# A two-block transformer kernel on one core: the engines' queues laid by the context's timeline simulation

## The chip, the cores and the metric

The kernel runs on one core of a Trainium2 chip. Its time is the device time in microseconds (us) of one execution. Three runs of the kernel before took 1210.09 to 1213.05 us, with a median of 1211.94.

The core has engines that work side by side, each with a queue that it takes from the front: PE (matrix multiplications and transposes; the load of the stationary operand is listed as PEld), DVE (vector engine), ACT (scalar engine), POOL (a second engine for vector steps) and SP, whose queue does nothing but start DMAs. An instruction waits at the front of its queue until its operands are there and its buffer is free, and everything queued behind it waits too.

## The reference, cut to what matters

Two blocks are applied to `x` (512 tokens, 1024 wide, float32). The first one modulates the normalised input by a condition vector `c`, projects it, and runs two attentions with eight heads each:

```
mod = silu(c) @ w_ada + b_ada                      # shift, scale, gate
h = rms_norm(x, g_pre) * (1 + scale) + shift
qa, ka, va, fa, za, qb, kb, vb, zb = split(h @ w_in)
oa = forgetting_attention(qa, ka, va, fa) * silu(za)          # "fox"
ob = sliding_window_sink_attention(rope(qb), rope(kb), vb) * silu(zb)
x = x + gate * rms_norm(concat(oa, ob) @ w_out, g_post)
```

The second has three branches (a gated convolution with 31 taps, a differential attention with eight heads, a cross attention to 256 memory rows), merged by gates:

```
h = rms_norm(x, norm_g);  mem_h = rms_norm(mem, mem_norm_g)
u = silu(layer_norm(conv31(a * sigmoid(b)))) * silu(c_gate);   y_conv = u @ w_conv
a = softmax(q1 k1 + alibi) - lam * softmax(q2 k2 + alibi);     y_diff = (norm(a @ v) * silu(d_gate)) @ w_diff
y_mem = (softmax(norm(x_q) norm(k_mem)) @ v_mem * silu(x_gate)) @ w_x
x = x + (g0 * y_conv + g1 * y_diff + g2 * y_mem) @ w_out
```

## The kernel before, in words

*Matmuls in three passes.* Float32 products are split into a high and a low half and multiplied as high by high, high by low and low by high. The input `h` lies transposed in `hh` and `hl`. Each weight chunk goes through `load_w` (L158 to L176): a DMA from SP's queue into one of three `raw` buffers (L164), a rounding copy `wh` on ACT (L170), and the rest `wl = raw - wh` on DVE, every fourth one on POOL (L172). The matmuls read `wh` and `wl`: L198 with the weight as stationary operand (256-column chunks, outputs of 128 by 512 in transposed layout), L215 with `h` stationary (512-column chunks, natural layout), L207 for the keys of the sliding attention.

*The opening.* The memory keys (L421, `mem_k`, two halves of 16 matmuls each) and values (L431, `mem_v`) are products of the memory rows. The modulation is eight loads of 1 MB (`ada`, L328), each turned into column sums on DVE (`gemv`, L335 to L338), summed over the partitions by two tiny matmuls (L442) and made into a shift and a scale (`mod` L445, `gs` L446) with which ACT and POOL write one eighth of `hh` and `hl` (L448 to L450). The memory keys are normalised by a chain of ten small DVE steps (L228 to L237) and scaled (L512).

*The attentions.* In the first block the sliding attention has scores `sc` (L688, L689), transposes `tp` (L710) and products `pv` (L727); the fox attention L768 and L769, L784, L807, with DVE steps L771, L775, L787 and L813 between them; a row of gate sums (L751) is woven in. In the second block the differential attention has L1043 and L1044, L784, L1077, the cross attention L1187, L1208, L1230; its queries are normalised by POOL (`xqn`, L987) and transposed (L284). The 240 steps of the convolution (L933) are given to DVE at low priority. The gates, the projections of the branches and the output follow as long rows of L198 and L215.

*What sets the order.* The code emits instructions in an order of its own: a `Fill` object weaves pieces of the projections between the steps of the attentions. That order is a priority, which `low()` raises or lowers by a number for a part of the code (the convolution taps, the memory keys' scaling, small constants). The queues are then laid by the tile context: it goes through the instructions with a model of how long each one takes, and appends to each engine's queue the one of highest priority among those whose operands the model holds to be there. Which instruction stands ahead of which in a queue thus depends on the durations and waits of that model. The tile pools set how far an engine may run ahead: three banks for matmul outputs, two each for scores and transposes, one for attention products.

The context is opened in one line (L1471), which encloses the whole kernel function.

## Time and profile before

| | |
|---|---|
| median of 3 runs | 1211.94 us (1210.09 to 1213.05) |
| the profiled execution | 1207.46 us |
| its span, first to last instruction | 1205.6 us |
| mean granted clock of PE | 0.989 |
| PE, DVE, ACT, POOL busy | 1145.5, 920.8, 552.1, 206.7 us |
| DMA | 165.25 MB, 137 GB/s |

The span is what the profiler recorded between the first and the last instruction; the execution is slightly longer. Busy times are sums over an engine's instructions, so an idle engine shows as the difference to the span, but not why it idles: for that the waits are read, which name for each gap the event that ended last. The granted clock is the share of full speed (2.4 GHz) that PE was given.

### The profile page before, as it was taken

The page shows a single profiled execution, that of the slowest core. Times are in us where ns is not written, and L with a number is a line of the kernel's source. Part 1 is how long each engine was busy: PE and PEld are TensorE (multiplying, and loading weights), DVE is VectorE, ACT ScalarE, POOL GpSimd, SP SyncE. Part 2 cuts the span into 40 slices and gives each one's busy share as a digit, 9 for nine tenths or more (in the row PEclk, how much of TensorE's full clock was granted, in tenths as well). Part 3 has the DMA queues.
Part 4 walks back from the last instruction along what each step waited for, and adds up shares of the span by engine and source line. Part 5 has one row for each costly group of instructions (what it writes and reads, how often), then busy time and mean ns, then how long its engine had stood idle before and what let it go on. Part 6 is the DMA issues. An engine that isn't in the chain of part 4 may idle for free. (4 is left out here: it accounts for less than half of the span.)

```text
span 1205.6 us, 16186 instructions
## 1 busy us (share of the span) xinstructions
PE 1145.5 (95%) x5584; PEld 938.3 (78%) x5584; DVE 920.8 (76%) x2004; ACT 552.1 (46%) x1157; POOL 206.7 (17%) x158
## 2 busy tenths in 40 slices
PE   6979999999899999998999999989999999999998
PEld 3557787777677878887898787868788888888887
DVE  5597677789887699999999979978884488453342
ACT  4554567547665354444545443444432245242230
POOL 0534200000121212020111211121101131110110
PEclk9989999999999999999999899999999999999999
DMA  9475421353474423323233333233335856422232
GB/s 351 152 247 189 126 88 63 130 161 89 141 243 140 123 70 97 100 93 114 88 115 105 114 114 127 101 114 123 111 134 180 298 177 228 145 90 96 97 112 98
DMA packets 59873, 165.25 MB, mean 137 GB/s; under 512 B 7088, under 2 KB 11440, under 8 KB 58768
## 3 DMA queue, kind: packets, MB, share of 16 engines
q1 hardware_dynamic: 35824, 122.41, 30.9%
q10 hardware_dynamic: 23968, 41.82, 9.7%
q8 instruction: 44, 0.72, 0.2%
q14 instruction: 37, 0.30, 0.1%
HBM read 136.80 MB, written 20.58 MB: 131 GB/s over the span
## 5 line engine op out<-in xcount | busy, mean ns | idle before, releaser
L170 ACT CAST wh<-raw 128x512 fp32r<-128x512 f32 (+1 forms) x360 | 214.9, 616 | 195.5 <-PE mm L198 115.0
L172 POOL TENSOR_TENSOR wl<-raw,wh 128x512 fp32r<-128x512 f32 (+1 forms) x94 | 137.4, 1462 | 831.2 <-ACT wh L170 776.4
L172 DVE TENSOR_TENSOR wl<-raw,wh 128x512 fp32r<-128x512 f32 (+1 forms) x266 | 194.1, 745 | 91.7 <-ACT wh L170 88.2
L198 PE MATMUL mm<-hh,wh 128*128 128x512 f32 x640 | 255.7, 400 | 0.0
L198 PE MATMUL mm<-hh,wl 128*128 128x512 f32 x640 | 251.8, 393 | 0.0
L198 PE MATMUL mm<-hl,wh 128*128 128x512 f32 x640 | 251.6, 393 | 0.0
L933 DVE SCALAR_TENSOR_TENSOR cv<-u,vec,cv 128x512 f32<-128x512 f32 x240 | 195.1, 813 | 3.1
L198 PEld LDWEIGHTS mm<-hh,wl 128*128 128x128 f32 x640 | 121.4, 190 | 25.4
L198 PEld LDWEIGHTS mm<-hh,wh 128*128 128x128 f32 x640 | 121.5, 190 | 23.7
L198 PEld LDWEIGHTS mm<-hl,wh 128*128 128x128 f32 x640 | 121.4, 190 | 23.4
L215 PE MATMUL mm<-wh,hh 128*128 128x512 f32 x256 | 102.7, 401 | 0.6 <-ACT qkn L973 0.3
L215 PE MATMUL mm<-wh,hl 128*128 128x512 f32 x256 | 100.2, 391 | 0.0
L215 PE MATMUL mm<-wl,hh 128*128 128x512 f32 x256 | 100.1, 391 | 0.0
L198 PE MATMUL mm<-bh,wh 128*128 128x512 f32 x192 | 75.2, 392 | 0.0
L198 PE MATMUL mm<-bh,wl 128*128 128x512 f32 x192 | 74.7, 389 | 0.0
L198 PE MATMUL mm<-bl,wh 128*128 128x512 f32 x192 | 74.7, 389 | 0.0
L1048 ACT ACTIVATE dp<-dp,dst 128x128 f32<-128x128 f32 (+3 forms) x64 | 35.6, 558 | 70.3 <-DVE dst L1046 70.2
L215 PEld LDWEIGHTS mm<-wh,hh 128*128 128x128 f32 x256 | 48.2, 188 | 11.1 <-ACT qkn L973 1.0
L215 PEld LDWEIGHTS mm<-wh,hl 128*128 128x128 f32 x256 | 48.1, 188 | 10.4
L215 PEld LDWEIGHTS mm<-wl,hh 128*128 128x128 f32 x256 | 48.2, 188 | 9.1 <-DVE wl L172 0.3
L207 PE MATMUL mm<-wl,hh 128*128 128x256 f32 (+1 forms) x160 | 46.8, 293 | 4.9 <-DVE wl L172 4.9
L207 PE MATMUL mm<-wh,hl 128*128 128x256 f32 (+1 forms) x160 | 46.3, 290 | 0.0
(330 smaller groups left out, 2110.1 us busy)
## 6 DMA issues: line engine op xcount, KB each, us to landing
raw<-in_w_dram SPq DMA_DIRECT2D x88, 512.0 KB, 3.7
raw<-in_w_out_dram SPq DMA_DIRECT2D x24, 512.0 KB, 3.7
raw<-in_w2n_dram SPq DMA_DIRECT2D x24, 512.0 KB, 3.4
ada<-in_w_ada_dram SPq DMA_DIRECT2D x8, 1024.0 KB, 6.1
rawm<-in_w_mem_dram SPq DMA_DIRECT2D x8, 512.0 KB
raw<-in_w_mem_dram SPq DMA_DIRECT2D x8, 512.0 KB
raw<-in_w1n_dram SPq DMA_DIRECT2D x8, 512.0 KB, 4.3
ada<-in_w_gate_dram SPq DMA_DIRECT2D x8, 512.0 KB, 4.3
```

Source lines behind the costliest of these rows:

```text
L170: act.copy(out=wh, in_=raw[:, s])
L172: eng.tensor_tensor(out=wl, in0=raw[:, s], in1=f(wh), op=ALU.subtract)
L198: m = pe.matmul(out=ps, lhsT=a[:, c0:c0 + P], rhs=at(b, k), start=(n == 0 and i == 0), stop=(n == KT - 1 and i == 2))
L207: pe.matmul(out=ps, lhsT=at(a, k)[:, t * P:(t + 1) * P], rhs=b[:, 0:n], start=(start and m == 0 and i == 0), stop=(stop and m == len(order ...
L215: pe.matmul(out=ps, lhsT=at(a, k)[:, t * P:(t + 1) * P], rhs=b[:, 0:n], start=(m == 0 and i == 0), stop=(m == KT - 1 and i == 2))
L933: dve.scalar_tensor_tensor(out=a, in0=u[:, j:j + S], scalar=dw[:, m * 31 + j:m * 31 + j + 1], in1=a, op0=ALU.mult, op1=ALU.add)
L1048: act.activation(out=p_[:, :w], in_=p_[:, :w], func=AF.Exp, scale=-1.0, bias=st_[:, 0, n, m:m + 1], accum_out=st_[:, 1, n, m:m + 1])
```

## The change: another model lays the queues

The tile context is told to use its timeline simulation as the model when it lays the queues.

```diff
--- before.py
+++ after.py
@@ -1468,7 +1468,7 @@
     arrays = {f"in_{k}_dram": np.ascontiguousarray(v) for k, v in _layout(inputs).items()}
     aps = {k[3:-5]: nc.dram_tensor(k, a.shape, mybir.dt.from_np(a.dtype), kind="ExternalInput").ap() for k, a in arrays.items()}
     out = nc.dram_tensor("out_0_dram", (NT, P, 1024), F32, kind="ExternalOutput").ap()
-    with tile.TileContext(nc) as tc:
+    with tile.TileContext(nc, schedule_with_timeline_sim=True) as tc:
         two_block_kernel(tc, aps, out)
     r = run_bass_kernel_spmd(nc, [arrays], core_ids=[0])
     got = r.results[0]["out_0_dram"]
```

Instructions, operands, loads and buffers stay what they were: the same matrix instructions, the same 289 entries of SP's queue, the same steps on DVE, the same weights. Of 1887 buffers in the on-chip memory 225 get another address. What differs is the place of instructions in the queues. Three places follow; numbers behind a name tell tiles of one name apart, and x2 means two such rows in a run.

SP's queue in the opening, where the last loads of the modulation weights (`ada`), of the memory values (`raw` from w_mem) and the first chunk for the sliding attention's keys (`raw` from w1c) meet. Before:

```order
L328 DMA ada_321<-in_w_ada_dram 128x2048
L328 DMA ada_363<-in_w_ada_dram 128x2048
L164 DMA raw_580<-in_w_mem_dram 128x1024
L164 DMA raw_590<-in_w_mem_dram 128x1024
L328 DMA ada_365<-in_w_ada_dram 128x2048
L328 DMA ada_367<-in_w_ada_dram 128x2048
L164 DMA raw_783<-in_w1c_dram 128x528
L164 DMA raw_793<-in_w1c_dram 128x528
L164 DMA raw_803<-in_w1c_dram 128x528
L164 DMA raw_813<-in_w1c_dram 128x528
```

Now:

```order
L328 DMA ada_321<-in_w_ada_dram 128x2048
L164 DMA raw_580<-in_w_mem_dram 128x1024
L328 DMA ada_363<-in_w_ada_dram 128x2048
L164 DMA raw_590<-in_w_mem_dram 128x1024
L164 DMA raw_783<-in_w1c_dram 128x528
L164 DMA raw_793<-in_w1c_dram 128x528
L164 DMA raw_803<-in_w1c_dram 128x528
L328 DMA ada_365<-in_w_ada_dram 128x2048
L328 DMA ada_367<-in_w_ada_dram 128x2048
L164 DMA raw_813<-in_w1c_dram 128x528
```

The loads ada_365 and ada_367 have moved behind three of the four loads of w1c, and ada_363 behind raw_580.

PE's queue in the sliding attention, at the scores of its seventh block (sc_1941 to sc_1956, tokens of one block against keys), the transposes of the block before (tp_1979, tp_1986, of spt_1860) and a product (pv_1969). Before, with a gate projection (mm_1924) around:

```order
L688 MATMUL sc_1946<-kb11_1205,qs_1723 128x256
L689 MATMUL sc_1946<-kbl1_1206,qs_1723 128x256
L727 MATMUL pv_1969<-sph_1900,vbh_781 64x512
L727 MATMUL pv_1969<-spl_1901,vbh_781 64x512
L688 MATMUL sc_1951<-kb11_1205,qs_1731 128x256
L689 MATMUL sc_1951<-kbl1_1206,qs_1731 128x256
L727 MATMUL pv_1969<-sph_1900,vbl_782 64x512
L688 MATMUL sc_1956<-kb11_1205,qs_1734 128x256
L689 MATMUL sc_1956<-kbl1_1206,qs_1734 128x256
L710 MATMUL tp_1979<-cst_79,spt_1860 128x128 x4
L710 MATMUL tp_1986<-cst_79,spt_1860 128x128 x4
```

Now, with a projection of the fox attention's values (mm_2274) around:

```order
L215 MATMUL mm_2274<-wh_2158,hl_84 128x512
L688 MATMUL sc_1946<-kb11_1205,qs_1723 128x256
L689 MATMUL sc_1946<-kbl1_1206,qs_1723 128x256
L710 MATMUL tp_1979<-cst_79,spt_1860 128x128
L710 MATMUL tp_1986<-cst_79,spt_1860 128x128
L710 MATMUL tp_1979<-cst_79,spt_1860 128x128
L710 MATMUL tp_1986<-cst_79,spt_1860 128x128
L710 MATMUL tp_1979<-cst_79,spt_1860 128x128
L710 MATMUL tp_1986<-cst_79,spt_1860 128x128
L710 MATMUL tp_1979<-cst_79,spt_1860 128x128
L710 MATMUL tp_1986<-cst_79,spt_1860 128x128
L688 MATMUL sc_1951<-kb11_1205,qs_1731 128x256
```

The four scores no longer stand together; pv_1969 has gone ahead of them, the transposes of the earlier block come between sc_1946 and sc_1951, and the bulk matmuls ahead are those of a later chunk.

PE's queue in the cross attention, at the transposes (tp_8248, tp_8255) of the normalised queries xqn_7879. Before, in the midst of the gate projection mm_8233:

```order
L198 MATMUL mm_8233<-hh_83,wl_8157 128x512
L198 MATMUL mm_8233<-hh_83,wh_8156 128x512
L198 MATMUL mm_8233<-hl_84,wh_8156 128x512
L284 MATMUL tp_8248<-cst_79,xqn_7879 128x128 x2
L284 MATMUL tp_8255<-cst_79,xqn_7879 128x128 x2
L198 MATMUL mm_8233<-hh_83,wl_8157 128x512
L198 MATMUL mm_8233<-hh_83,wh_8160 128x512
L284 MATMUL tp_8248<-cst_79,xqn_7879 128x128 x2
L284 MATMUL tp_8255<-cst_79,xqn_7879 128x128 x2
L198 MATMUL mm_8233<-hl_84,wh_8160 128x512
```

Now, in the midst of a later one, mm_8353:

```order
L198 MATMUL mm_8353<-hh_83,wh_8284 128x512
L198 MATMUL mm_8353<-hl_84,wh_8284 128x512
L198 MATMUL mm_8353<-hh_83,wl_8285 128x512
L284 MATMUL tp_8248<-cst_79,xqn_7879 128x128 x2
L198 MATMUL mm_8353<-hh_83,wh_8290 128x512
L198 MATMUL mm_8353<-hl_84,wh_8290 128x512
L198 MATMUL mm_8353<-hh_83,wl_8291 128x512
L198 MATMUL mm_8353<-hh_83,wh_8290 128x512
L198 MATMUL mm_8353<-hl_84,wh_8290 128x512
L284 MATMUL tp_8255<-cst_79,xqn_7879 128x128
L284 MATMUL tp_8248<-cst_79,xqn_7879 128x128 x2
L284 MATMUL tp_8255<-cst_79,xqn_7879 128x128 x3
```

The rest of mm_8233, a whole further output (mm_8298) and the first half of mm_8353 have moved ahead of the transposes.

## Rows read from the trace of the kernel before

**Rows 1.** The page, part 1: busy us and share of the span.
```profile
PE 1145.5 (95%) x5584; PEld 938.3 (78%) x5584; DVE 920.8 (76%) x2004; ACT 552.1 (46%) x1157; POOL 206.7 (17%) x158
```

**Rows 2.** Windows by stage: length, busy per engine (instructions), clock, DMA share, GB/s.
```profile
0.00:105.00 105.00, 81.94 (x338) 56.30 (x338) 74.53 (x190) 52.52 (x101) 33.78 (x40) 0.95 0.68 248
105.00:215.70 110.70, 108.96 (x538) 86.80 (x537) 82.41 (x218) 66.97 (x166) 21.58 (x20) 1.00 0.31 98
215.70:321.00 105.30, 101.16 (x521) 79.46 (x522) 95.28 (x299) 64.16 (x158) 8.21 (x6) 1.00 0.37 118
321.00:451.60 130.60, 124.12 (x624) 102.67 (x624) 102.03 (x216) 68.18 (x136) 22.97 (x20) 1.00 0.47 156
451.60:724.20 272.60, 261.76 (x1429) 225.70 (x1428) 260.34 (x616) 129.69 (x286) 47.33 (x28) 0.98 0.33 105
724.20:870.00 145.80, 135.55 (x673) 113.01 (x671) 128.82 (x220) 62.05 (x129) 22.10 (x13) 0.98 0.33 113
870.00:1206.00 336.00, 331.99 (x1472) 274.34 (x1470) 177.40 (x250) 108.53 (x186) 50.77 (x33) 1.00 0.45 150
```

**Rows 3.** Chain of waits, its last pieces: start us, us, what.
```profile
995.23 163.25 PE mm L198 x720
1158.47 43.53 PE mm L215 x192
```

**Rows 4.** Waits of PE: us in total, times, longest.
```profile
PE tp L284 <- POOL xqn L987: 4.9, 1, 4.9
...
PE mm L207 <- DVE wl L172: 4.9, 2, 2.9
...
PE sc L442 <- DVE acc L338: 3.5, 2, 2.8
...
PE sc L1187 <- DVE xl L1119: 2.7, 1, 2.7
```

**Rows 5.** Windows at low clock behind 450, columns as in Rows 2.
```profile
471.80:475.20 3.40, 3.40 (x10) 2.61 (x10) 3.40 (x15) 1.31 (x4) 0.92 (x1) 0.52 0.10 12
686.80:693.60 6.80, 5.72 (x17) 5.04 (x18) 6.72 (x16) 3.17 (x8) 0.00 (x0) 0.51 0.21 81
802.90:806.30 3.40, 3.27 (x12) 2.43 (x12) 1.29 (x2) 0.97 (x2) 1.65 (x1) 0.52 0.25 95
857.50:860.90 3.40, 3.34 (x8) 2.66 (x9) 3.38 (x7) 1.06 (x3) 0.00 (x0) 0.52 0.01 5
```

**Rows 6.** Timeline of SP's queue, 69 to 88: start us, us, what.
```profile
69.74 3.89 SPq L328 DMA_DIRECT2D ada<-in_w_ada_dram  x2
73.72 14.16 SPq L164 DMA_DIRECT2D raw<-in_w1c_dram  x4
```

**Rows 7.** The page, part 6: KB of one, us to landing.
```profile
ada<-in_w_ada_dram SPq DMA_DIRECT2D x8, 1024.0 KB, 6.1
```

**Rows 8.** Timeline of DVE: start us, us, operation, [idle before, releaser].
```profile
48.72 0.16 DVE L445 SCALAR_TENSOR_TENSOR mod<-sc,vec 128x2 f32<-128x2 f32 x1 [9.19 <-PE sc L442]
...
74.66 1.76 DVE L172 TENSOR_TENSOR wl<-raw,wh 128x512 fp32r<-128x512 f32 x1
...
79.64 3.49 DVE L337 SCALAR_TENSOR_TENSOR acc<-ada,cs,acc 128x256 f32<-128x256 f32 x6
...
95.19 2.05 DVE L512 TENSOR_SCALAR mk<-mk,ry 128x256 f32<-128x256 f32 x8
...
1161.04 0.68 DVE L172 TENSOR_TENSOR wl<-raw,wh 128x512 fp32r<-128x512 f32 x1
```

**Rows 9.** Timeline of PE, opening and cross attention.
```profile
34.35 14.00 PE L421 MATMUL mm<-rawm,mT 128*128 128x512 f32 x32
...
802.75 0.87 PE L284 MATMUL tp<-cst,xqn 128*128 128x128 f32 x4 [4.91 <-POOL xqn L987]
```

**Rows 10.** Timeline of POOL at the same two places.
```profile
73.19 2.69 POOL L450 TENSOR_TENSOR hl<-ht,hh 128x512 fp32r<-128x512 f32 x2 [4.02 <-ACT hh L449]
...
799.82 4.73 POOL L987 TENSOR_TENSOR xqn<-xqn,ry 128x1024 f32<-128x1024 f32 x2 [6.11 <-DVE ry L237]
```

## The prediction

> **What bounds the kernel now.** I read the page's busy line first [rows 1]: the matrix engine (PE) is busy 1145.5 of 1205.6 us, the vector engine (DVE) 920.8, and no other engine comes near. The average hides that the stages differ, so the second view cuts the span where one stage hands over to the next [rows 2]. In each row the reader subtracts PE's busy time from the length: 23.1 us idle up to 105, 1.7 up to 215.7, 4.1 up to 321, 6.5 up to 451.6, 10.8 up to 724.2, 10.3 up to 870. DVE is as full as 95.28 of 105.3 in the third row and 260.34 of 272.6 in the fifth: there two engines are close to their limits at once. The last row's 4.0 us are the two ends of a stretch without gaps: the chain of waits closes with two unbroken pieces of matmuls, 163.25 and 43.53 us [rows 3]. 720 matmuls in 163.25 us are 226.7 ns each, and no order of the same matmuls shortens that. An order can win only what lies ahead of 870.
>
> PE's waits say who was late [rows 4]: a POOL normalisation (4.9 in one go), DVE's low half of a weight chunk (4.9 in two), the opening's matrix-vector sums (3.5) and an operand of the cross attention (2.7) are four of some three dozen kinds. Last I read the granted clock: for 3.4, 6.8, 3.4 and 3.4 us PE was granted 0.51 to 0.52, 1.2 instead of 2.4 GHz [rows 5]; the third of these stretches begins where PE came out of its longest wait behind 100 [rows 9]. In 17.0 us a share of 0.48 is lost, 8.2 us: 4.9 of it up to 724, 3.3 behind. A wait removed there can give more than its length.
>
> **The change part by part.** No instruction, byte or buffer is added or taken away; only the place in each engine's queue differs, so the cost is all in who waits at the head of a queue. I summed the durations of the traced execution along the old and the new queues and compared, for producers and consumers, the work queued ahead of each; figures of queued work below are such sums.
>
> *From 870 on* the queues are the same but for a few exchanged rows: 0, at most 1 either way.
>
> *The opening, up to 105.* PE's first scale sum (L442) no longer stands behind all 16 matmuls of the second key product but behind 8; DVE had idled 9.19 us for just this sum [rows 8], and at 14.00 us for 32 such matmuls [rows 9] 8 of them are 3.5 us. The memory keys' rsqrt and scaling (L228 to L237, L512) leave the place where they held up a weight chunk: L512 alone is 2.05 us [rows 8], and PE's waits on that chunk's low half were 4.9 [rows 4]. Against that, the last two loads of the modulation weights (ada_365, ada_367) go behind three loads of w1c on SP's queue. Before, they went out at 69.74, and the four of w1c took from 73.72 to 87.88, since each needs a buffer to come free [rows 6]. If the third still goes out at about 81, a 1 MB load of 6.1 us [rows 7] lands at 87, and two sums of 8 products, six of which are 3.49 us [rows 8] (4.6 a sum with the two first and the last), end at 96; before, one was through its six at 83.13, and 4.6 for the other make 87.7. Below: all these waits go, 3.5 + 4.9, say 9 earlier. Above: DVE is 8.3 later, of which the 4.9 that PE waited anyway are covered: 3.4 later. I take 3 earlier, nearer to the row of the idle DVE, since the buffers for w1c should come free earlier too.
>
> *Sliding and fox attention, 105 to 321.* PE's new queue puts bulk matmuls ahead of the small attention steps: the scores sc_1951 stand behind 21.6 us more of PE work, the last product of the sliding attention (pv_2094) behind 14.1 more. DVE idles 28.3 us from 105 to 215.7 [rows 2], so a later score costs nothing there. From pv_2094 to the last fox product (pv_3268) DVE then has 95.4 us queued and PE only 88.0, where it was 94.5 and 101.2. PE comes to pv_2094 at 215.7 + 14.1 - 3 (opening) - 1.7 (its waits) = 225, DVE some 3 us ahead of it, and needs 95.4: 317.4 at best, with the idle of before (10.0) 327.4. Before: 321. The opening's gain is thus none of its own; it pays for this. Up to 321 together I take 2 earlier, from 9 earlier to 8 later.
>
> *321 to 451.6* hardly moves; PE's 6.5 us of waits stay: 0, 2 either way.
>
> *Differential attention, 451.6 to 724.2.* Here the same lag helps: transposes and products move behind 14 to 23 us more of PE work, the DVE steps that feed them behind 11 to 22. PE's 10.8 us of waits and 4.9 of clock are to be had, 15.7. But DVE has 265.7 us queued from the first to the last of these products, where the row of before shows 260.34 in 272.6: 6.9 us of room, so PE can have more than that only by what it was laid ahead. I take 7, nearest to this room, from 1 to 15.
>
> *Cross attention, 724.2 to 870.* The longest wait goes: the transposes of xqn_7879 waited 4.91 us until 802.75 [rows 9] for POOL's two steps of 4.73 us, begun at 799.82 [rows 10], and stand now behind 11.2 us more of matmuls; with its clock (half of 3.3) 6.5 us. Another weight split is put ahead of that POOL step, far less than 11.2. The scores that waited 2.7 for xl go the other way: xl stands behind 24 us more of DVE work, the scores behind 8.6 more of PE's. From the first differential product to there DVE has 307.6 us queued and PE 311.0, so PE meets its operand by 3 us if DVE never idles, and waits if it does. Of 13.6 us of waits and clock I take 5, from 3 later to 12.
>
> The Trainium skill, "SBUF — State Buffer" (Who interferes with whom), says that DVE and POOL share one pair of ports and that the second to issue fully blocks until the first ends. The trace agrees: DVE's 128x512 subtraction takes 0.68 us at 1161.04 and 1.76 at 74.66 [rows 8], beside two POOL steps of 2.69 together [rows 10]. If an order is laid by durations without that block, it is too tight where DVE has least room; ten new meetings in the fifth stage, at 1.08 us each, would take 11 us, more than its 6.9 of room, and the gain there would be nil.
>
> **Sum.** 0 - 2 - 0 - 7 - 5 = -14 us: 1207.5 becomes 1193.5 for a profiled execution. The median of the runs shown (1211.9) is 4.5 above the profiled one, so 1198. The squares of the parts' half widths (8, 2, 7, 7.5) add to 13 us: the likeliest case reaches from 1185 to 1211.
>
> **The rivals.**
> (a) The waits come back under other names. DVE's in-order queue now holds steps that wait for PE's later scores (its place lags PE's by 10 to 18 us at 160 to 215, by 2 to 5 in 440 to 700). For it: DVE's 260.34 of 272.6. Against: the lag is one shift, not one at each step, and PE's queue is as much ahead. The fifth stage gives 2, the sixth 2, the front 0: 1208.
> (b) Slower: DVE becomes what PE waits for. If DVE idles as long as before (10.0 us in the third row of the stages, 12.3 in the fifth) while its queue there has grown, the fox stage ends at 327.4, 6.4 late, the differential one takes 265.7 + 12.3 = 278.0, 5.4 more, and the last waits stay: 1207.5 + 11.8 + 4.5 = 1224. It decides from where DVE's idle time in the two passes 16.8 us (377.9 less 361.1 queued). Against: DVE waits less if PE has nothing to wait for.
> (c) More: the waits from 105 to 870 shrink to a third (33.4 x 2/3 = 22), the clock stays up (8), the opening gives its 9, less what DVE can't follow, some 8: 31 less, 1181. For it: by the same sums nearly every small PE step from 325 to 870 has 3 to 10 us of other work between its operand and itself, where before it had 0.1.
> (d) The waits only trade places and PE's matmuls alone set the end: within 3 us of 1212. Against it stand 33.4 us of idle time in stretches whose order moves by 10 to 20 us.
>
> **How the numbers follow.** A run here tells 0.3%, 3.6 us, from no change. Forecast (1198) 0.47, (a) 0.15, (b) 0.20, (c) 0.12, (d) 0.06. Faster: 0.45 of the forecast, 0.12 of (c), 0.08 of (a), 0.65. Within: 0.06 of (d), 0.07 of (a), 0.02 of the forecast, 0.15. Slower: 0.20, (b). The range leaves out most of (b) and the lower end of (c): 1179 to 1216.
>
> **What would show it.** Right: from 451.6 to 870 PE's idle falls from 21 to some 10 us; the wait of L284 for xqn is gone and, with it, the stretch of half clock behind it; L198's last piece and L215's keep their 163 and 44 us; DVE's idle ahead of its first L445 falls from 9.2 to some 5.7. Wrong: PE waits on the fox attention's DVE steps (L771, L787, L813) for more than 10 us; DVE waits for ada at 80 to 87 and L215's first matmul begins later than 104.65; or PE's waits in the differential stage are as many as before under other names.

## The result, and the profile after

The changed kernel takes 1197.33 us (median of 4 runs, 1195.91 to 1198.98) against 1211.59 us (4 runs) of the kernel before: a ratio of 0.9883, interval 0.9862 to 0.9904, 14.3 us less. Predicted were 1198, in a range from 1179 to 1216. The profiled execution took 1195.91 us, its span is 1194.1 us. The sum came out almost exactly, but its terms did not: the opening and what lies behind the fox attention gave more than said, the two attentions between them cost more. The experiments take the sum apart.

The busy line and the granted clock, in 40 slices, of the kernel after, and last the clock of before ([rows 1] has its busy line): PE has the same work and 12 us less idle time, but the clock has new dips in the eighth and tenth slice.

```profile
PE 1146.4 (96%) x5584; PEld 940.9 (79%) x5584; DVE 910.0 (76%) x2004; ACT 551.1 (46%) x1157; POOL 206.4 (17%) x158
...
PEclk9989999897999999999999999999999999999999
```

```profile
PEclk9989999999999999999999899999999999999999
```

Four of the windows of [rows 2] (first, third, fifth and sixth):

```profile
0.00:105.00 105.00, 90.48 (x383) 64.74 (x384) 76.62 (x207) 57.86 (x110) 41.25 (x44) 0.95 0.74 269
215.70:321.00 105.30, 93.18 (x435) 70.78 (x436) 89.75 (x280) 58.83 (x142) 8.45 (x6) 0.89 0.42 131
451.60:724.20 272.60, 266.69 (x1462) 229.49 (x1461) 266.89 (x634) 132.97 (x299) 47.75 (x29) 0.99 0.34 107
724.20:870.00 145.80, 144.64 (x740) 122.22 (x739) 131.62 (x242) 66.68 (x137) 23.61 (x15) 1.00 0.36 122
```

PE's busy time is now 90.48 of 105 in the opening (81.94 before), 93.18 of 105.3 in the third stage (101.16) and 411.33 of 418.4 in the two last (397.31). The opening and the two last rows gained, the third stage lost, and of these stretches it is the only one, in the two traces, with a mean clock below 0.9. (The cuts are at the same times; the stages themselves lie up to 13 us earlier and later.)

The chain still ends as in [rows 3], the shorter first piece being one of 711 matmuls:

```profile
985.75 161.21 PE mm L198 x711
1146.96 43.53 PE mm L215 x192
```

Of PE's waits in [rows 4], those for xqn, for L172 at L207 and for xl are gone. The one of L442 has grown from 3.5 to 4.9, and so have those of the fox attention and of the gate row, from 1.7 to 4.5 and from 0.5 to 2.8 (an excerpt of after; the last line is of before):

```profile
PE sc L442 <- DVE acc L338: 4.9, 2, 2.5
PE sc L768 <- DVE fst L771: 4.5, 8, 2.6
...
PE tp L751 <- DVE ptl L787: 2.8, 1, 2.8
```

```profile
PE sc L768 <- DVE fst L771: 1.7, 2, 1.3
```

The granted clock behind 200, as in [rows 5]: two long stretches at 1.2 GHz, 10.5 and 14 us, in the sliding and fox attention, where before had none, and one of 3.5 us behind 450, where before had 17 (one of 3.4 at 385 is not shown).

```profile
217.50:228.00 10.50, 8.19 (x23) 4.82 (x21) 5.22 (x16) 5.26 (x15) 0.00 (x0) 0.51 0.36 125
279.00:293.00 14.00, 9.91 (x33) 6.22 (x33) 13.40 (x50) 4.26 (x10) 0.00 (x0) 0.51 0.55 167
658.00:661.50 3.50, 3.48 (x15) 2.94 (x14) 3.44 (x12) 2.62 (x8) 0.00 (x0) 0.51 0.02 5
```

In the opening, SP's queue (as in [rows 6]) sent the three loads of w1c from 57.97 on and the two of ada at 65.54, 4 us earlier than before, not at 81:

```profile
57.97 6.15 SPq L164 DMA_DIRECT2D raw<-in_w1c_dram  x3
65.54 4.39 SPq L328 DMA_DIRECT2D ada<-in_w_ada_dram  x2
```

DVE's first scale step waits 0.74 us and stands at 36.55, 12.2 us earlier than in [rows 8]. The price is in a later sum over ada, a wait of 2.44 us for the load:

```profile
36.55 0.16 DVE L445 SCALAR_TENSOR_TENSOR mod<-sc,vec 128x2 f32<-128x2 f32 x1 [0.74 <-PE sc L442]
...
78.56 1.79 DVE L335 TENSOR_SCALAR acc<-ada,cs 128x256 f32<-128x256 f32 x2 [2.44 <-DMA ada<-in_w_ada_dram]
```

The transposes of xqn (as in [rows 9, 10]): POOL ends at 806.55, PE comes to them at 806.93 and does not wait. The 11.2 us of matmuls that the prediction counted ahead of them were just enough.

```profile
802.35 4.20 POOL L987 TENSOR_TENSOR xqn<-xqn,ry 128x1024 f32<-128x1024 f32 x2 [2.96 <-DVE ry L237]
```

```profile
806.93 0.38 PE L284 MATMUL tp<-cst,xqn 128*128 128x128 f32 x2
```

How the new dip looks from inside: PE from 275.20 to 285, in the fox attention, columns start, us, operation, and in brackets the idle time ahead and who ended it. There is not one bulk matmul (L198, L215) in it; PE waits for a DVE step, does small ones at half clock, and waits again.

```profile
275.20 0.33 PE L768 MATMUL sc<-k,qs 128*128 128x384 f32 x1
275.37 0.34 PE L769 MATMUL sc<-k,q 68*128 68x384 f32 x1
275.55 0.38 PE L784 MATMUL tp<-cst,fp 128*128 128x128 f32 x2
278.74 0.46 PE L751 MATMUL tp<-acc,cst 128*128 128x128 f32 x2 [2.81 <-DVE ptl L787]
279.52 0.80 PE L768 MATMUL sc<-k,qs 128*128 128x512 f32 x1 [0.31 <-DVE fst L771]
280.11 0.63 PE L769 MATMUL sc<-k,q 68*128 68x512 f32 x1
280.80 0.87 PE L784 MATMUL tp<-cst,fp 128*128 128x128 f32 x3
284.32 0.47 PE L768 MATMUL sc<-k,qs 128*128 128x128 f32 x1 [2.65 <-DVE fst L771]
284.59 0.41 PE L769 MATMUL sc<-k,q 68*128 68x128 f32 x1
285.05 0.79 PE L751 MATMUL tp<-acc,cst 128*128 128x128 f32 x2
```

Of DVE's queue at the second of these waits two lines, start and us: the softmax step L771 that PE waits for stands behind a step of other keys (L564). Ahead of it, from 281.66 on, DVE does a step of the queries (L277) and two of the gate sums (L753, L337); DVE itself does not idle here.

```profile
282.97 0.69 DVE L564 TENSOR_TENSOR k<-mm,k 64x512 fp32r<-64x512 f32 x1
283.70 0.56 DVE L771 CUSTOM_DVE_ANT_0 fp<-sc,cst 128x384 f32<-128x384 f32 x1
```

In the queues this is a count: between the last matmul of pv_2574 and the first of pv_2975 (the products of the fox attention's second and fourth head in either trace) stood 76 bulk matmuls before, and now 7. At 226.7 ns each, 69 are 15.6 us of work that PE had beside the softmax steps there and does elsewhere instead.

### The profile page after: what moved, and what is told of

It reads as the page before. It is cut to its first block, busy times and chain, and to the rows that moved or that the text cites. A ratio compares the mean times of both kernels' runs of the same rounds, so it can differ in the third digit from the quotient of the medians.

```text
span 1194.1 us, 16211 instructions
## 1 busy us (share of the span) xinstructions
PE 1146.4 (96%) x5584; PEld 940.9 (79%) x5584; DVE 910.0 (76%) x2004; ACT 551.1 (46%) x1157; POOL 206.4 (17%) x158
## 4 chain that ended last, share of the span: by engine, by line
PE 70%; DVE 21%; DMA 4%; issue 3%; ACT 2%; POOL 0%; SPq 0%; ACTq 0%; DVEq 0%
PE mm L198 42%; PE mm L215 13%; DVE cv L933 5%; DVE wl L172 2%; PE mm L207 2%; PE mm L421 2%; DVE acc L337 2%; PE pv L807 1%; DVE dp L1046 1%; DVE ptl L787 1%; PE pv L727 1%; DMA raw<-in_w_out_dram 1%; PE sc L1187 1%; PE pv L1230 1%; PE tp L284 1%
## 5 line engine op out<-in xcount | busy, mean ns | idle before, releaser
L172 POOL TENSOR_TENSOR wl<-raw,wh 128x512 fp32r<-128x512 f32 (+1 forms) x94 | 136.2, 1450 | 872.3 <-ACT wh L170 809.1
L172 DVE TENSOR_TENSOR wl<-raw,wh 128x512 fp32r<-128x512 f32 (+1 forms) x266 | 188.5, 720 | 88.2 <-ACT wh L170 87.6
L198 PE MATMUL mm<-hh,wh 128*128 128x512 f32 x640 | 251.7, 393 | 0.0
L198 PE MATMUL mm<-hh,wl 128*128 128x512 f32 x640 | 251.0, 392 | 0.0
L198 PE MATMUL mm<-hl,wh 128*128 128x512 f32 x640 | 250.8, 392 | 0.0
L198 PEld LDWEIGHTS mm<-hh,wl 128*128 128x128 f32 x640 | 120.3, 188 | 24.3
L198 PEld LDWEIGHTS mm<-hh,wh 128*128 128x128 f32 x640 | 120.3, 188 | 23.7
L198 PEld LDWEIGHTS mm<-hl,wh 128*128 128x128 f32 x640 | 120.3, 188 | 23.5
L215 PE MATMUL mm<-wh,hh 128*128 128x512 f32 x256 | 101.1, 400 | 2.9 <-DVE vl L544 1.7
L215 PE MATMUL mm<-wh,hl 128*128 128x512 f32 x256 | 101.3, 398 | 1.0 <-DVE hl L858 1.0
L215 PE MATMUL mm<-wl,hh 128*128 128x512 f32 x256 | 101.5, 397 | 0.1
L198 PE MATMUL mm<-bh,wh 128*128 128x512 f32 x192 | 75.2, 392 | 0.0
L198 PE MATMUL mm<-bh,wl 128*128 128x512 f32 x192 | 74.7, 389 | 0.0
L198 PE MATMUL mm<-bl,wh 128*128 128x512 f32 x192 | 74.7, 389 | 0.0
L215 PEld LDWEIGHTS mm<-wh,hh 128*128 128x128 f32 x256 | 48.7, 190 | 13.8 <-DVE vl L544 2.5
L215 PEld LDWEIGHTS mm<-wh,hl 128*128 128x128 f32 x256 | 48.4, 189 | 10.7 <-DVE hl L858 1.4
L215 PEld LDWEIGHTS mm<-wl,hh 128*128 128x128 f32 x256 | 48.7, 190 | 10.0 <-DVE wl L172 0.5
L207 PE MATMUL mm<-wh,hh 128*128 128x256 f32 (+1 forms) x160 | 47.2, 297 | 1.2 <-ACT hh L449 1.0
L207 PE MATMUL mm<-wl,hh 128*128 128x256 f32 (+1 forms) x160 | 46.9, 295 | 0.0
```

Source lines behind the costliest of these rows:

```text
L172: eng.tensor_tensor(out=wl, in0=raw[:, s], in1=f(wh), op=ALU.subtract)
L198: m = pe.matmul(out=ps, lhsT=a[:, c0:c0 + P], rhs=at(b, k), start=(n == 0 and i == 0), stop=(n == KT - 1 and i == 2))
L207: pe.matmul(out=ps, lhsT=at(a, k)[:, t * P:(t + 1) * P], rhs=b[:, 0:n], start=(start and m == 0 and i == 0), stop=(stop and m == len(order ...
L215: pe.matmul(out=ps, lhsT=at(a, k)[:, t * P:(t + 1) * P], rhs=b[:, 0:n], start=(m == 0 and i == 0), stop=(m == KT - 1 and i == 2))
```

## The experiments

All of them use one tool: order dependencies without a wait that pin chosen instructions of an engine in a listed order, added when the kernel is traced and before the queues are laid. Everything else is laid anew by the context's model, around them, and need not come out in the order of either kernel. Each time is compared with runs of the kernel before on the same chip; the intervals reach 2 to 4 us to either side, so that a difference of that size between two rows is none.

```diff
+PINS = (
+    (
+        "1362+2 1367+2 1390 1372+2 1391+2 1377+2 1393+21 1422+2 1427+2 ...
...
+def pin(tc, nc):
...
+    for chain, ahead, behind in PINS:
+        q = list(names(chain))
+        for a, b in zip(q, q[1:]):
+            tc.add_manual_dep(by[b], a, no, reason="issue order")
...
+        for b in names(behind):
+            tc.add_manual_dep(by[b], q[-1], no, reason="issue order")
...
         two_block_kernel(tc, aps, out)
+        pin(tc, nc)
```

(`chain` is the listed order; what is in `behind` is queued after its last instruction.) In the short diffs below `window(engine, first, last)` stands for such a table, from the first instruction of one line to the last of another, in the order of the kernel that is named.

| | queues | us | ratio to before (interval) |
|---|---|---|---|
| changed | all by timeline simulation | 1197.3 | 0.9883 (0.9862 to 0.9904) |
| e1 | changed, PE's attentions of before | 1189.4 | 0.9820 (0.9802 to 0.9838) |
| e2 | changed, PE of before up to the fox attention's end | 1190.4 | 0.9831 (0.9810 to 0.9851) |
| e3 | changed, all of PE of before | 1224.1 | 1.0105 (1.0082 to 1.0127) |
| e4 | before, all of PE of changed | 1231.7 | 1.0176 (1.0149 to 1.0202) |
| e5 | changed, PE, DVE, ACT, SP in the attentions of before | 1176.3 | 0.9710 (0.9682 to 0.9739) |
| e6 | before, opening of changed | 1198.2 | 0.9898 (0.9867 to 0.9928) |
| e7 | before, transposes of xqn moved | 1204.4 | 0.9942 (0.9920 to 0.9965) |
| e8 | before, DVE's first 36 steps of changed | 1206.2 | 0.9965 (0.9943 to 0.9987) |
| e9 | changed, DVE's attentions of before | 1223.9 | 1.0110 (1.0075 to 1.0145) |
| e10 | e1 and the gate sums on DVE | 1191.5 | 0.9843 (0.9817 to 0.9869) |
| e11 | changed, PE and DVE in the attentions of before | 1185.2 | 0.9776 (0.9748 to 0.9803) |
| e12 | changed, PE, ACT and SP in the attentions of before | 1188.1 | 0.9809 (0.9779 to 0.9840) |

"The attentions" are the sliding and the fox attention, from L688 to the last L807.

**e1, e2: PE's queue of before in part.**

```diff
+PINS = (window("PE", "L688", "L807"),)      # e1, order of before
+PINS = (window("PE", start, "L807"),)       # e2, order of before
```

> The changed kernel, with PE's queue from the first scores of the sliding attention (L688) to the last fox product (L807, pv_3268) held in the order of before; opening and everything behind as changed. Theory (stages add up: against before the changed kernel gains some 10 to 14 us in the opening, loses some 25 in sliding and fox attention because bulk matmuls were laid ahead of the small steps and are missing beside them, and gains some 22 behind): the 25 come back, about 1173 us (1170 to 1181). Rival (DVE, with 95 us queued in that stretch and 98 per cent busy behind it, is the bound, so that PE's order there is no matter): 1190 to 1197.

Measured: 1189.4, far from the theory and at the edge of its rival. With PE's queue of before in this stretch 8 of the 21 to 25 us come back. The expectation has the other engines as changed there, and that they were not: lined up row by row by line and tile, DVE's steps in the stretch agree with those of before to about 59 per cent and with those of the changed kernel to about 31.

> The changed kernel, with PE's queue from the start to the last fox product (pv_3268) in the order of before; behind it as changed. Theory (the gain of some 22 us behind 325 is that stretch's own): 1189 us (1185 to 1194). Rival (that gain is only DVE catching up what it was late by in the fox stage, so nothing is to be caught up here): 1203 to 1211.

Measured: 1190.4, as the theory had it. The gain behind the fox attention is that stretch's own and no catching up.

**e3, e4: PE's whole queue exchanged.**

```diff
+PINS = (window("PE", start, end),)   # e3 in the changed kernel, order of before; e4 in before, order of the changed
```

> The changed kernel with the whole of PE's queue in the order of before; DVE, ACT, POOL and SP laid by the timeline simulation around it. Theory (PE's order is the cause): 1211 us (1206 to 1216). Rival (the order of DVE, POOL and SP is): 1195 to 1201.

> The kernel before with the whole of PE's queue in the order of the changed one; the other engines laid by the model of before around it. Theory (PE's order is the cause): 1197 us (1192 to 1202). Rival (the order of the other engines is): 1207 to 1215.

Measured: 1224.1 and 1231.7, slower than both kernels, which neither theory nor rival had. PE's order alone brings neither kernel's time. Whether the others' order would is not shown: around a pinned PE queue they came out as in neither kernel (behind the fox attention DVE's steps in e3 agree to about 66 per cent with before and to 48 with the changed kernel). In e3 the waits behind 340 grew, as this excerpt of PE's waits from 340 to 870 shows (total, times, longest); before, the first of these pairs had 0.6, the last 4.9:

```profile
PE tp L258 <- DVE rdiag L252: 7.2, 2, 3.9
PE tp L258 <- DVE rt L234: 6.3, 1, 6.3
...
PE tp L284 <- POOL xqn L987: 5.5, 1, 5.5
```

**e5, e6: whole stages exchanged, all engines together.** The queues then agree with one kernel in one stage and with the other in the rest: from there on each engine's queue is that of the changed kernel (e5) or of before (e6), to a few rows. These two mixes are clean: in the opening, in the attentions and behind, the rows of PE, DVE and ACT in the traces agree to about 99 per cent with the kernel that they are meant to follow.

```diff
+PINS = (                                    # e5, order of before
+    window("PE", "L688", "L807"), window("DVE", "L690", "L813"),
+    window("ACT", "L692", "L811"), window("SP", "L652", "L566"),
+)
+PINS = (                                    # e6, in the kernel before, order of the changed
+    window(each of the five engines, start, ahead of the sliding attention),
+)
```

> The changed kernel with the queues of PE, DVE, ACT and SP in sliding and fox attention (first scores to the last product of the fox attention) in the order of before; opening and everything behind as changed. Theory (the loss of some 25 us there is that of the joint new order, of which PE's queue alone gave back 8): all of it comes back, 1174 us (1170 to 1180). Rival (the stretch costs what it costs because DVE has 95 us to do in it; the rest of the loss stays): 1185 to 1191.

> The kernel before with the queues of all five engines in the opening (up to the first scores of the sliding attention) in the changed order; everything behind as before. Theory (what the opening gives stays given): 1201 us (1199 to 1204). Rival (my prediction's view that the fox stage is bound by DVE and uses the gain up): 1208 to 1212.

Measured: 1176.3 and 1198.2, both on the theory's side, and e6 even beyond. The opening gives 12.3 us (1210.5 to 1198.2), the attentions cost 21.0 (1176.3 to 1197.3), the rest gives 21.9 (1198.2 to 1176.3). That these three make 13.2 less (the direct comparison has 14.3) is no test, since each step starts where the last one ended. The traces hold the test: the start of the last product of the fox attention, in before, after, e5 and e6:

```profile
323.19 0.22 PE L807 MATMUL pv<-pth,vl 128*64 128x128 f32 x1
```

```profile
333.11 0.22 PE L807 MATMUL pv<-pth,vl 128*64 128x128 f32 x1
```

```profile
314.56 0.22 PE L807 MATMUL pv<-pth,vl 128*64 128x128 f32 x1
```

```profile
314.49 0.22 PE L807 MATMUL pv<-pth,vl 128*64 128x128 f32 x1
```

From there to the end of the spans (1205.6, 1194.1, 1176.0, 1195.8) it takes 882.4, 861.0, 861.4 and 881.3 us. In its new order the rest thus takes 861 us behind attentions of either order, 20 to 21 less than in the old one; the new opening brings the last product 8.7 earlier, whatever follows; and between after and e5 the attentions cost 18.6. So the stages add up. (The opening's 8.7 stands beside the 12.3 of the medians because the profiled execution of before, 1207.5, was 3 us below the median of e6's runs of before.) e5 beats both kernels: 34 us below before, 21 below the changed one. Its busy line and clock:

```profile
PE 1137.7 (97%) x5584; PEld 936.3 (80%) x5584; DVE 911.7 (78%) x2004; ACT 550.4 (47%) x1157; POOL 206.0 (18%) x158
...
PEclk9989999999999999999999999999999999999999
```

Two stretches side by side show the terms, columns as in [rows 2]. They are cut at the same times, so they hold somewhat different work. Before:

```profile
200.00:340.00 140.00, 133.54 (x684) 104.47 (x683) 118.89 (x356) 86.56 (x214) 13.32 (x10) 1.00 0.41 133
450.00:870.00 420.00, 398.91 (x2108) 340.11 (x2106) 390.76 (x842) 193.12 (x417) 69.43 (x41) 0.98 0.33 107
```

After:

```profile
200.00:340.00 140.00, 122.04 (x587) 92.25 (x586) 112.95 (x355) 79.48 (x201) 9.29 (x7) 0.91 0.35 110
450.00:870.00 420.00, 412.93 (x2208) 353.04 (x2207) 400.12 (x879) 201.25 (x439) 71.79 (x44) 1.00 0.35 112
```

e5:

```profile
200.00:340.00 140.00, 133.78 (x674) 105.31 (x674) 119.02 (x350) 85.10 (x204) 13.07 (x10) 1.00 0.46 141
450.00:870.00 420.00, 412.76 (x2174) 352.04 (x2173) 397.77 (x857) 197.56 (x424) 72.59 (x43) 1.00 0.36 115
```

From 200 to 340 PE idles 6.5 us before, 18.0 after and 6.2 in e5, and is at half clock for 0, 24.5 and 0 us, of which it is busy 18.1 (8.19 and 9.91, above). That is 11.5 us of idle and 18.1 x 0.49 = 8.9 of clock, together 20 for the 21 measured. From 450 to 870 it idles 21.1, 7.1 and 7.2 us, and is at half clock for 17.0, 3.5 and 3.5 us, busy for 15.7 of them before ([rows 5]) and 3.5 after: 14.0 us of idle and 15.7 x 0.48 - 3.5 x 0.49 = 5.8 of clock, together 20 for the 21.9. In e6 the second stretch is that of before again, while the first keeps its clock:

```profile
200.00:340.00 140.00, 133.79 (x673) 104.96 (x672) 118.82 (x350) 83.63 (x201) 13.35 (x10) 1.00 0.46 144
450.00:870.00 420.00, 399.10 (x2086) 339.40 (x2086) 384.42 (x834) 194.20 (x418) 64.62 (x39) 0.98 0.34 108
```

**e7: one move.**

```diff
+PINS = (("8354+12 8249+2 8256+2 8251+2 8258+2 ", "", ""),)
```

(8354 and the next eleven are the first half of mm_8353, the others the eight transposes of xqn_7879.)

> The kernel before with one move: the eight transposes of xqn_7879 (L284) behind the first 12 matmuls of mm_8353, where the changed kernel has them. Theory (the wait of 4.9 us and the stretch of half clock behind it go): 1205 us (1204 to 1207). Rival (another wait takes its place, since the cross attention's scores behind the transposes come later too): 1209 to 1213.

Measured: 1204.4, 6.1 us less than the 1210.5 of before (by the interval 4 to 10); the theory. In the trace PE idles 16.0 us from 450 to 870 instead of 21.1, and the stretch at half clock right behind the transposes is gone (the next one is at 854). They stand without a wait:

```profile
810.21 1.04 PE L284 MATMUL tp<-cst,xqn 128*128 128x128 f32 x8
```

**e8: another small move.**

```diff
+PINS = (window("DVE", start, first "L237"),)      # order of the changed
```

> The kernel before with only the first 36 steps of DVE's queue in the changed order (scaling of the transposed memory rows, L409, ahead of the constants and the angle steps). Theory (PE's wait of 3.9 us at 9 us goes and stays gone): 1207 us (1206 to 1209). Rival (later waits of the opening for DVE and for loads swallow it): 1210 to 1212.

Measured: 1206.2, 4.3 us less (by the interval 2 to 7); the theory. PE's first matmuls in e8, 13 transposes in one run, where before waited 3.90 us ahead of the last four (the last line is from the waits of before):

```profile
7.36 3.24 PE L405 MATMUL mm<-cst,mt 128*128 128x128 f32 x13 [0.55 <-DMA mt<-in_mem_dram]
10.39 4.92 PE L421 MATMUL mm<-rawm,mT 128*128 128x512 f32 x9
```

```profile
PE mm L405 <- DVE mT L409: 3.9, 1, 3.9
```

The changed kernel does the same: its 13 transposes begin at 7.31 and take 2.79 us.

**e9 to e12: which engine lost the 21 us in the attentions.**

```diff
+PINS = (window("DVE", "L690", "L813"),)                                  # e9
+PINS = (window("PE", "L688", "L807"), gate sums among the fox steps)     # e10
+PINS = (window("PE", "L688", "L807"), window("DVE", "L690", "L813"))     # e11
+PINS = (window("PE", ...), window("ACT", ...), window("SP", ...))        # e12
```

> The changed kernel with DVE's queue alone, from the first step of the sliding attention (L690) to the last of the fox attention (L813), in the order of before; PE and the others are laid around it. Theory (of the 21 us that the stretch lost, 13 are DVE's order, which puts gate sums and weight halves ahead of the fox attention's softmax steps, 8 are PE's): 1184 us (1181 to 1188). Rival (a mixed order loses, as both whole mixes did): 1192 to 1200.

> The kernel with PE's sliding and fox attention as before (1189) and, added to it, the gate sums on DVE (L335 to L338, L752, L753) held in their places of before among the fox attention's softmax steps (L771, L774, L775, L787); weight halves, ACT and SP as changed. Theory (the gate sums ahead of the softmax steps are most of the 13 us left): 1177 us (1175 to 1181). Rival (the output chunk's weight halves, ACT's or SP's order are): 1185 to 1190.

> The changed kernel with the queues of PE and DVE in sliding and fox attention in the order of before; ACT and SP are laid around them. Theory (PE and DVE hand each other every softmax step, so their two orders together are all that matters, and DVE's weight halves and value halves, not its gate sums, made the difference): 1176 us (1174 to 1180), as with all four. Rival (ACT's copies or SP's loads set it): 1183 to 1190.

> The changed kernel with the queues of PE, ACT and SP in sliding and fox attention in the order of before; DVE is laid around them. Theory (DVE's order is what is still missing): 1189 us (1185 to 1193), as with PE alone. Rival (ACT's or SP's order set it): 1174 to 1180.

Measured: e9 1223.9, 26.5 us slower than the changed kernel, worse than its rival. The first of PE's waits from 180 to 360 and the stretch of the windows above:

```profile
PE sc L768 <- DVE fst L771: 7.4, 8, 2.5
PE pv L807 <- ACT pth L786: 4.8, 4, 2.1
PE pv L727 <- DVE spl L713: 4.6, 4, 2.7
```

```profile
200.00:340.00 140.00, 117.64 (x518) 90.23 (x517) 97.61 (x320) 66.11 (x169) 6.95 (x5) 0.85 0.28 88
```

PE idles 22.4 us there at a mean clock of 0.85, and its queue was laid anew in an order of neither kernel. The same stretch of e1:

```profile
200.00:340.00 140.00, 126.08 (x618) 98.34 (x618) 107.75 (x324) 76.52 (x187) 10.62 (x8) 0.96 0.41 124
```

In e1 the bulk matmuls are back between the small steps, all 76 of them, and PE still idles 13.9 us, 7.7 more than in e5, with DVE's steps of the softmax and of the gate sums (L774, L338) as the longest of its waits. So to put the bulk matmuls back is not enough. e10 took 1191.5, a little above its rival: the gate sums are not what e1 still lacked; that theory fell. e11 took 1185.2, as its rival had it (ACT or SP matter too), e12 1188.1, as its theory had it: beside PE's queue, DVE's brings 4 us, ACT's and SP's bring 1, which the intervals hardly tell from nothing, and both together 13. No queue that was tried alone gives back the 21 us; some 8 of them (13 less 4 and 1) come back only when all four queues are those of one kernel. Which of ACT's copies or SP's loads it takes was not tried.

## Why the prediction was right, and where it was wrong

*The tail and the mechanism.* The tail kept its 43.53 us and its unbroken run, as the first view had it, and the gain is from waits and from the clock that went with them. In the stretch from 451.6 to 870 PE's idle fell from 21.1 to 7.1 us (some 10 were said).

*The opening: 3 earlier said, 12.3 measured (e6).* The step that failed is the bound on the loads of ada. It took the third load of w1c to go out at 81; its buffers came free earlier, as the memory values did, whose last matmul (L431) PE began 15 us earlier (67.73 instead of 82.80), and ada went out before 70. The first scale sum came 12.2 us earlier and not 3.5, since all that PE does ahead of it moved up too. And the wait of 3.90 us at 9, for the steps of DVE that scale the transposed memory rows, was left out of the sum altogether: constants of no urgency stood ahead of them (e8: 4.3 us). By the traces alone, e6 against before, the opening gives 8.7.

*"The opening's gain is thus none of its own; it pays for this."* Wrong. In e6 the last matmul of the fox attention (L807) stands at 314.49 instead of 323.19, 8.7 earlier, and the gain is there at the end. When that stage starts earlier, with its own order kept, it ends earlier.

*The attentions: with the opening 2 earlier, at most 8 later, said; 8.7 later measured (21.0 of loss less 12.3).* The last fox product came 9.9 later than before (its last matmul 333.11 instead of 323.19), where 3.6 earlier to 6.4 later were given. The step compared sums of work, DVE's 95.4 with PE's 88.0, and took the larger one. But in this stage PE and DVE hand each small step to one another, and neither sum is the bound: from 215.7 to 321 DVE too idles more, 15.6 us instead of 10.0. What PE has beside the small steps while it waits is bulk matmuls; 69 of them stood elsewhere in the new order. PE then waits for single steps, and falls to 1.2 GHz, a term that was counted only where the trace of before had it. But PE's old order, with these matmuls in their places, gave back only 8 us (e1); the other 13 came with the queues of DVE, ACT and SP as well (e5), and which of their steps it takes stays open. The Trainium skill, "TensorE: Matmul & The Clock Gate" (Part 1), says that the engine's clock is lowered when the engine isn't kept busy; the trace agrees: 0.51 from 279 to 293, with PE busy 9.91 of 14 us, right behind a wait of 2.81.

*Differential and cross attention: 12 said, 21.9 measured.* The mechanism was right, the size of one term was not. In the window of the differential attention PE has 4.9 us less idle time and 3 less of clock, 8 where 7 were said, and DVE took up 6.6 of its 6.9 us of room (266.89 busy instead of 260.34). In that of the cross attention, 724.2 to 870, it is 9.1 us of idle and 3.3 of clock, 12 where 5 were taken of 13.6. The step that failed is the wait for xl that was allowed for: laid behind 24 us more of DVE's work, it came in time, and no wait of L1187 is left. The single wait of xqn was sized right: 6.5 us said, 6.1 measured alone (e7).

*The rivals.* (a) and (d) didn't come. Of (b) one half did, in that the fox stage ended 9.9 late where (b) had 6.4, though not because DVE was full, and its 5.4 in the differential stage did not. (c) names what the rest of the kernel did. The rule of the Trainium skill, "SBUF — State Buffer" (Who interferes with whom), that DVE and POOL block one another shows no added loss here: the 266 steps of L172 on DVE took 720 ns in the mean after and 745 before.

*The signs.* Of the signs that would show it right, PE's idle time from 451.6, the wait for xqn and the last pieces came as said; DVE's wait ahead of its first L445 fell further, to 0.74 instead of 5.7. Of those that would show it wrong, PE's waits for DVE in the fox attention are 9.5 us (4.5 for L771; 2.8, 1.2 and 1.0 for L787, from 230 to 345), just under the 10 named; DVE did wait for ada, 2.44 us, but L215 began at 94.12 and not behind 104.65. The sign in the fox attention was the right place to look, and its clock was missing from it.

So the median was met by luck: an opening and a rest that gave 19 us more than said were set off by attentions that took 20 us more, and no step of the prediction made the two cancel (by stages: 12.3 - 3 and 21.9 - 12, against 21.0 - 1).

## What to carry to other kernels

A new order is a set of queues that fit one another: sums of work along one engine say little, and so does one engine's queue with the others laid anew around it, since they come out in a third order. Exchange whole stages with all engines, see which gains, and keep each stage's better order (here 21 us below the better of the two kernels). Where a planner brings bulk work forward, ask what it leaves beside the small steps later, and add a clock term there, since the trace of before doesn't have it. A list of waits from the old trace is worth reading from the first one on: the 3.9 us at 9 us stood in it and came back (4.3 us, e8).

## What the runs showed of the hardware

The granted clock differs much between the kernels: from the first to the last instruction of each profiled execution, PE was granted 1.2 GHz for 17 us in e5 (1176.3 us), 27 before, 41 after, 58 in e3 (1224.1), 68 in e9 (1223.9) and 75 in e4 (1231.7). It goes with the time at both ends and does not rank the kernels between (after is faster than before). Short waits close together cost nearly as much again in clock, though none of them is long: 11.5 us of idle time and 8.9 of clock from 200 to 340, where the longest single wait is 2.81.
